# Sums of the down products' right operands formed in DRAM by accumulating transfers

## The chip, the cores and the metric

The kernel runs on one core of one Trainium2 chip. The metric is the device time of one execution in microseconds, lower being better; the time given for the kernel before is the median of three runs. The profile is of one further execution.

## The reference

One inference step of a hybrid decoder layer. What matters here are its two feed-forward halves, each over 1048 (first) or 1032 (second) tokens, with 1024 model dimensions and 2816 hidden features; everything is float32:

```python
def swiglu(x, wg, wu, wd):
    return (jax.nn.silu(x @ wg) * (x @ wu)) @ wd
...
    h = h + 0.5 * swiglu(rmsnorm(h, n1), w1g, w1u, w1d)
...
    h = h + 0.5 * swiglu(rmsnorm(h, n2), w2g, w2u, w2d)
```

Between the two stand an input projection, two recurrent scans (HGRN2 and Mamba-2) and an output projection. They are the same in both kernels.

## The kernel before, in words

Every large product is made of three TensorE passes (`mm3`, lines 166 to 171): both operands are split into a high part that TensorE can take exactly and a low rest, and high x high, high x low and low x high are added up. On top of that the FFN products are formed by a scheme of seven block products in place of eight: an operand is cut into two by two blocks, and the seven left and right operands are blocks or sums of blocks.

An FFN runs in `ffn` as a list of steps, each a chain of nine or twelve matmuls. `S.before(i, fn)` puts `fn`'s instructions ahead of step i, and this hand-made order holds for TensorE, VectorE, ScalarE and SyncE. GpSimd's queue is not in that list; its order follows the program.

**Gate and up products.** Eleven pairs i = 0 to 10 of 128-feature columns f = 2i and 2i + 1. `Plain` and `pair` make the first ones, `two_pairs` the other nine, each in 24 product steps of twelve matmuls and seven shorter chains of six. At a pair's end VectorE multiplies silu(gate) by up. That gives four gated blocks of 128 partitions by 524 columns: (f even, token half 0), called block 1; (f even, half 1), block 12; (f odd, half 0), block 2; (f odd, half 1), block 3. They are made at lines 621, 713 and 906, in two `s` buffers per pair.

**Right operands of the down products.** The seven operands are blocks 1, 2, 3 and the sums 5 = 12 - 1, 6 = 3 - 5, 7 = 3 - 12 and 4 = 2 - 6. `Hidden` keeps them in seven DRAM tensors, one for each operand. Per pair VectorE makes the four sums with `tensor_sub` (line 991) into two more `s` buffers, and SyncE stores all seven operands (line 994), 256 rows of 262 (or 258) floats each. `jobs` and `jobs_apart` place these: for the pairs of `two_pairs` the subtractions stand at steps s0 + 26, 32, 36 and 38, the stores at s0 + 19 to 41, so that some of them lie in the next pair or, for the last pair, in the first steps of the down products.

**Down products.** `down` runs through the operands in the order 1, 5, 6, 7, 3, 4, 2, with 24 steps for each. An operand is loaded from DRAM in three groups of pairs (0 to 3, 4 to 7, 8 to 10) and two token quarters (line 1023), cast on ScalarE (1027) and its rest formed on VectorE (1031). The down weights are loaded at line 1074, summed at 1084, split at 1089 and 1094. The first operand's products are evacuated by ScalarE (1114), those of the others are added by VectorE (1118), with a factor 0.5. SyncE issues its transfers strictly in order, so a store that waits for VectorE holds the loads behind it.

Of the kernel before, what the change touches and what calls it, by code (L numbers as in the profile page):

```python
# [13 lines left out]
ALU = mybir.AluOpType  # L14
# [553 lines left out]
def halves(t):  # L568
    return t.rearrange("p (c t) -> p c t", c=2)


def pair(K, S, wg, wu, f, ops, spread, hid, late_r, tight, first=None):

    nc = K.nc
    fs = slice(f * P, f * P + P)
    s0 = len(S.steps)  # L580
    tm = {}
    left = Left(K, [wg[:, 0:4, fs], wu[:, 0:4, fs], wu[:, 4:8, fs], wg[:, 4:8, fs]], 4)

    def temp(n, cs):
        if n not in tm:
            tm[n] = halves(K.t(2 * K.Q))
        return tm[n][:, cs]

    def times_r(n, i, cs, src=None):
        t = temp(n, cs)  # L590
        nc.vector.tensor_mul(t, t if src is None else src, spread.lanes(i, cs))
        return t

    def post(p, cs, b):
        if p == 1:
            nc.scalar.copy(temp("z", cs), b)
        elif p == 6:
            nc.vector.tensor_add(temp("v", cs), b, temp("z", cs))
        elif p == 2 and f == 0:
            nc.scalar.copy(temp("g0", cs), b)  # L600
        elif p == 2:
            t = times_r("g0", 0, cs, b)
            nc.scalar.activation(t, t, AF.Silu)
        elif p == 5:
            nc.vector.tensor_add(temp("x", cs), b, temp("v", cs))
        elif p == 7:
            nc.vector.tensor_add(temp("u1", cs), b, temp("x", cs))
        elif p == 3:
            nc.vector.tensor_add(temp("g1", cs), b, temp("v", cs))
        else:  # L610
            nc.vector.tensor_add(temp("u0", cs), b, temp("v", cs))

    def silu(n, cs):
        t = times_r(f"g{n}", n, cs)
        nc.scalar.activation(t, t, AF.Silu)

    def product_(n, cs):
        if "h" not in tm:
            tm["h"] = True
            hid.append(K.slot("s", K.T))  # L620
        nc.vector.tensor_mul(halves(hid[0][:, n * 2 * K.Q : n * 2 * K.Q + 2 * K.Q])[:, cs], temp(f"g{n}", cs), temp(f"u{n}", cs))

    if not first:
        left.plan(S, s0, int(tight), 5 * int(tight))
        Unit(K, left.w, [o.op for o in ops], 4, post).both(S)
        cs = slice(0, 2)
        for i, (fn, *args) in enumerate(((silu, 1, cs), (times_r, "u1", 1, cs), (times_r, "u0", 0, cs), (product_, 0, cs), (product_, 1, cs))):
            S.before(s0 + 12 + i, lambda fn=fn, args=args: fn(*args))
        return

    late = {}

    def post_first(p, cs, b):

        if p == 5:
            late[p] = b
        else:
            post(p, cs, b)
            if p == 6:
                post(5, cs, late[5])  # L640

    order = first(S, left)
    unit = Unit(K, left.w, [o.op for o in ops], 4, post_first)
    for ps_ in (order[:6], order[6:]):
        for c in range(2):
            for p in (1, 5, 6, 7, 2, 3) if c and len(ps_) == 6 else ps_:
                unit.step(S, p, c, (c,), True)
    cs = slice(0, 2)
    for i, (fn, *args) in enumerate(((silu, 0, cs), (silu, 1, cs), (times_r, "u0", 0, cs), (product_, 0, cs), (times_r, "u1", 1, cs), (product_, 1, cs))):
        S.before(s0 + late_r + i, lambda fn=fn, args=args: fn(*args))  # L650


class Plain:
# [44 lines left out]
    def late(self, S, at):  # L698
        nc = self.K.nc
        cs = slice(0, 2)  # L700

        def silu(n):
            g = self.g[n]
            nc.vector.tensor_mul(g, g, self.spread.lanes(n, cs))
            nc.scalar.activation(g, g, AF.Silu)

        def scale(n):
            u = self.u[n]
            nc.vector.tensor_mul(u, u, self.spread.lanes(n, cs))

        def times(n):
            out = halves(self.box()[:, n * 2 * self.K.Q : n * 2 * self.K.Q + 2 * self.K.Q])
            nc.vector.tensor_mul(out, self.g[n], self.u[n])

        for i, (fn, n) in enumerate(((silu, 0), (silu, 1), (scale, 0), (times, 0), (scale, 1), (times, 1))):
            S.before(at + i, lambda fn=fn, n=n: fn(n))
# [138 lines left out]
def two_pairs(K, S, wg, wu, i, ops, spread, hids, sub, before):  # L855
# [6 lines left out]
    nc = K.nc  # L862
    s0 = len(S.steps) - (0 if before else 2)
# [39 lines left out]
    def out(f, n):  # L903
        if not hids[f]:
            hids[f].append(K.slot("s", K.T))
        nc.vector.tensor_mul(halves(hids[f][0][:, n * 2 * K.Q : n * 2 * K.Q + 2 * K.Q]), temp(f, f"g{n}"), temp(f, ("v", "u1")[n]))

    def post(f, p, c):
        if p == 1:
# [53 lines left out]
GROUPS = [(0, 4), (4, 4), (8, 3)]  # L963


class Hidden:


# [1 line left out]
        self.K = K  # L970
        self.d = {p: K.dram.tile([P, 2, FP, self.K.Q], F32, name=K.uid("hd")) for p in ORDER}

    def parts(self, i, hid):

        K = self.K
        t, b = {}, {}

        def block(n):

            return hid[n // 2][0][:, n % 2 * 2 * self.K.Q : n % 2 * 2 * self.K.Q + 2 * self.K.Q]  # L980

        def val(p):
            return b[p] if p in b else block({1: 0, 12: 1, 2: 2, 3: 3}[p])

        def sub(p, x, y):
            s = {5: 0, 6: 0, 7: 1, 4: 1}[p]
            if s not in t:
                t[s] = K.slot("s", self.K.T)
            o = (p in (6, 4)) * 2 * self.K.Q
            b[p] = t[s][:, o : o + 2 * self.K.Q]  # L990
            K.nc.vector.tensor_sub(b[p], val(x), val(y))

        def store(p):
            K.nc.sync.dma_start(self.d[p][:, :, i, :], halves(val(p)))

        return sub, store

    def jobs(self, S, i, hid, e0, e1):

        sub, store = self.parts(i, hid)  # L1000
        for at, args in zip((e0 + 10, e1 + 3, e1 + 5, e1 + 8), ((5, 12, 1), (6, 3, 5), (7, 3, 12), (4, 2, 6))):
            S.before(at, lambda args=args: sub(*args))
            S.before(at + 2, lambda p=args[0]: store(p))
        for at, p in ((e0 + 2, 1), (e1 + 2, 2), (e1 + 3, 3)):
            S.before(at, lambda p=p: store(p))

    def jobs_apart(self, S, i, hid, s0):

        sub, store = self.parts(i, hid)
        for d, args in zip((26, 32, 36, 38), ((5, 12, 1), (6, 3, 5), (7, 3, 12), (4, 2, 6))):  # L1010
            S.before(s0 + d, lambda args=args: sub(*args))
        for d, p in zip((19, 29, 32, 33, 35, 39, 41), (1, 5, 3, 2, 6, 7, 4)):
            S.before(s0 + d, lambda p=p: store(p))

    def load(self, S, p, at):

# [23 lines left out]
def down(K, S, wdv, hidden, src, h, after):  # L1040
# [68 lines left out]
    def post(p, j, cs, b):  # L1109
        if p == 1:  # L1110
            tiles(j)
            for i in range(2):
                for n in range(2):
                    nc.scalar.mul(hs[2 * j + i][:, cs, n], b, 0.5)
            return
        for i, n in {5: ((0, 1), (1, 1)), 6: ((0, 1), (1, 0), (1, 1)), 7: ((1, 0), (1, 1)), 3: ((0, 1),), 4: ((1, 0),), 2: ((0, 0),)}[p]:
            t = hs[2 * j + i][:, cs, n]
            nc.vector.scalar_tensor_tensor(t, b, 0.5, t, ALU.mult, ALU.add)  # L1118
        for i, n in {3: ((0, 1), (1, 1)), 4: ((1, 0),), 2: ((0, 0),)}.get(p, ()):
            if then:  # L1120
                for c in range(cs.start, cs.stop):
                    then(2 * j + i, 2 * c + n)
# [41 lines left out]
def ffn(K, wg, wu, wd, ops, spread, src, first, after, late_r, at, plain=False):  # L1164
# [10 lines left out]
    with K.tc.manual_schedule(engines={E.PE, E.DVE, E.Activation, E.SP}):  # L1175
# [3 lines left out]
        if plain:  # L1179
            hid = [[], []]  # L1180
            lefts = [Left(K, [w[:, k : k + 4, f * P : f * P + P] for w, k in ((wgv, 0), (wuv, 0), (wuv, 4), (wgv, 4))], 4) for f in range(2)]
            first(S, *lefts)
            for f in range(2):
                p = Plain(K, lefts[f], ops, spread, hid[f], f == 1)
                p.add(S)
                p.late(S, late_r + 6 * f)
            hidden.jobs(S, 0, hid, late_r + 2, late_r + 10)
        sub = SubBlocks(K, ops)
        sub.jobs(S, at)
        before = None  # L1190
        for i in range(int(plain), NF // 2):
            hid, e = [], []
            if i > 1:
                hid = [[], []]
                s0, before = two_pairs(K, S, wgv, wuv, i, ops, spread, hid, sub, before)
                hidden.jobs_apart(S, i, hid, s0)
                continue
            for f in (2 * i, 2 * i + 1):
                hid.append([])
                pair(K, S, wgv, wuv, f, ops, spread, hid[-1], late_r, f == (2 if plain else 1), first if f == 0 else None)  # L1200
                e.append(len(S.steps))
            hidden.jobs(S, i, hid, *([late_r + 2, e[1]] if i == 0 else e))
        h = []
        down(K, S, wdv, hidden, src, h, after)
        S.run()
# [1362 lines left out]
```

## Time and profile before

| | |
|---|---|
| median of three runs | 1922.09 us (1920.74 to 1922.73) |
| span of the profiled execution | 1920.9 us |
| TensorE busy | 1905.5 us (99%) |
| VectorE busy | 1526.5 us (79%) |
| ScalarE busy | 858.0 us (45%) |
| GpSimd busy | 30.1 us (2%) |
| hardware queue of the DMA engines | 255.79 MB, 43.1% of 16 engines |
| software queue of the DMA engines | 0.04 MB |

The median lies 1.2 us above the span, which counts from the first instruction to the last. In the views PE is TensorE, PEld its weight load, DVE VectorE, ACT ScalarE, POOL GpSimd, SP or SPq SyncE, which issues the transfers. L991 is line 991. The first FFN's gate/up stage runs to about 473 us, its down products to about 690; the scans follow; the second FFN's gate/up stage ends near 1680 and its down products close the program. A row of a table by stretch gives, for each engine, the busy time and in brackets the number of instructions, then TensorE's clock, the share of the 16 DMA engines and GB/s.

### The profile page before, as it was taken

The page shows a single profiled execution, that of the slowest core. Times are in us where ns is not written, and L with a number is a line of the kernel's source. Part 1 is how long each engine was busy: PE and PEld are TensorE (multiplying, and loading weights), DVE is VectorE, ACT ScalarE, POOL GpSimd, SP SyncE. Part 2 cuts the span into 40 slices and gives each one's busy share as a digit, 9 for nine tenths or more (in the row PEclk, how much of TensorE's full clock was granted, in tenths as well). Part 3 has the DMA queues.
Part 4 walks back from the last instruction along what each step waited for, and adds up shares of the span by engine and source line. Part 5 has one row for each costly group of instructions (what it writes and reads, how often), then busy time and mean ns, then how long its engine had stood idle before and what let it go on. Part 6 is the DMA issues. An engine that isn't in the chain of part 4 may idle for free.

```text
span 1920.9 us, 41195 instructions
## 1 busy us (share of the span) xinstructions
PE 1905.5 (99%) x16692; PEld 1875.2 (98%) x16692; DVE 1526.5 (79%) x2866; ACT 858.0 (45%) x1635; POOL 30.1 (2%) x88
## 2 busy tenths in 40 slices
PE   9999999999999999999999999999999999999998
PEld 9999999999999999999999999999999999999998
DVE  7888888889788877566585557999888888978974
ACT  6533333334534644466564545743333332453353
POOL 3000000000000000000000000000000000000000
PEclk9999999999999999999999999999999999999999
DMA  7143333335967541221463254133333333596852
GB/s 249 50 128 95 95 107 112 92 98 175 305 215 243 165 152 52 66 89 38 116 186 85 83 173 144 58 114 107 99 93 101 101 112 93 173 269 210 281 175 84
DMA packets 324209, 258.46 MB, mean 135 GB/s; under 512 B 18923, under 2 KB 298731, under 8 KB 324011
## 3 DMA queue, kind: packets, MB, share of 16 engines
q1 hardware_dynamic: 323779, 255.79, 43.1%
q8 instruction: 131, 2.15, 0.5%
q14 instruction: 59, 0.48, 0.1%
q0 software_dynamic: 224, 0.04, 0.0%
q10 hardware_dynamic: 16, 0.00, 0.0%
HBM read 190.79 MB, written 65.05 MB: 133 GB/s over the span
## 4 chain that ended last, share of the span: by engine, by line
PE 94%; DVE 3%; ACT 1%; issue 1%; DMA 0%; SPq 0%; DVEq 0%; ACTq 0%
PE acc L169 24%; PE acc L171 23%; PE acc L170 23%; PE mis L169 5%; PE mis L170 5%; PE mis L171 5%; PE mis L1963 1%; DVE u L382 1%; DVE u L367 1%; PE mis L1665 0%; PE mis L2030 0%; PE mis L1659 0%; DMA s<-in_x_prompt_dram 0%; PE mis L2055 0%; PE mis L1654 0%
## 5 line engine op out<-in xcount | busy, mean ns | idle before, releaser
L169 PE MATMUL acc<-u,ws 128*128 128x258 f32 (+4 forms) x3634 | 1064.0, 293 | 1.1 <-DVE u L1279 0.8
L171 PE MATMUL acc<-u,ws 128*128 128x258 f32 (+4 forms) x3634 | 1055.3, 290 | 0.7 <-DVE ws L501 0.7
L170 PE MATMUL acc<-u,ws 128*128 128x258 f32 (+4 forms) x3634 | 1054.8, 290 | 0.0
L169 PEld LDWEIGHTS acc<-u,ws 128*128 128x128 f32 x3634 | 686.5, 189 | 8.7 <-issue 6.2
L170 PEld LDWEIGHTS acc<-u,ws 128*128 128x128 f32 x3634 | 688.3, 189 | 0.8 <-DVE u L330 0.2
L171 PEld LDWEIGHTS acc<-u,ws 128*128 128x128 f32 x3634 | 686.1, 189 | 1.6 <-DVE ws L501 1.1
L169 PE MATMUL mis<-u,ws 128*128 128x262 f32 (+1 forms) x810 | 230.2, 284 | 0.0
L171 PE MATMUL mis<-u,ws 128*128 128x262 f32 (+1 forms) x810 | 228.7, 282 | 0.0
L170 PE MATMUL mis<-u,ws 128*128 128x262 f32 (+1 forms) x738 | 208.6, 283 | 0.0
L501 DVE TENSOR_TENSOR ws<-r,ws 128x512 fp32r<-128x512 f32 x266 | 181.6, 684 | 4.1 <-ACT ws L497 3.9
L901 ACT ACTIVATE t<-t 128x524 f32<-128x524 f32 (+1 forms) x72 | 46.1, 640 | 300.1 <-DVE t L898 300.1
L497 ACT CAST ws<-r 128x512 fp32r<-128x512 f32 x266 | 156.8, 615 | 42.2 <-PE mis L171 18.1
L169 PEld LDWEIGHTS mis<-u,ws 128*128 128x128 f32 x810 | 152.9, 189 | 0.1
L171 PEld LDWEIGHTS mis<-u,ws 128*128 128x128 f32 x810 | 152.7, 189 | 0.0
L170 PEld LDWEIGHTS mis<-u,ws 128*128 128x128 f32 x738 | 139.9, 190 | 0.1
L493 DVE TENSOR_TENSOR r<-r,r 128x512 f32<-128x512 f32 x150 | 100.8, 684 | 0.3
L1031 DVE TENSOR_TENSOR u<-u,u 128x1048 fp32r<-128x1048 f32 (+3 forms) x84 | 96.1, 1146 | 4.8 <-ACT u L1027 4.3
L1089 ACT CAST ws<-u 128x512 fp32r<-128x512 f32 (+1 forms) x72 | 42.1, 585 | 109.9 <-DVE u L1084 105.2
L164 DVE TENSOR_TENSOR ws<-r,ws 128x512 fp32r<-128x512 f32 x88 | 59.5, 685 | 38.3 <-ACT ws L163 38.0
L1027 ACT CAST u<-u 128x1048 fp32r<-128x1048 f32 (+3 forms) x84 | 82.8, 988 | 1.3 <-DMA u<-hd 1.3
L1118 DVE SCALAR_TENSOR_TENSOR s<-acc,s 128x524 f32<-128x524 f32 (+3 forms) x86 | 53.9, 651 | 35.3 <-PE acc L171 35.0
L898 DVE TENSOR_TENSOR t<-t,u 128x524 f32<-128x524 f32 (+1 forms) x108 | 73.2, 692 | 0.1
(465 smaller groups left out, 2329.1 us busy)
## 6 DMA issues: line engine op xcount, KB each, us to landing
r<-in_w_ffn_down_dram SPq DMA_DIRECT2D x128, 256.0 KB
hd<-s SPq DMA_DIRECT2D x93, 258.0 KB
r<-in_w_ffn_gate_dram SPq DMA_DIRECT2D x88, 256.0 KB
r<-in_w_ffn_up_dram SPq DMA_DIRECT2D x88, 256.0 KB
hd<-s SPq DMA_DIRECT2D x77, 262.0 KB
u<-hd SPq DMA_DIRECT2D x36, 516.0 KB
u<-hd SPq DMA_DIRECT2D x28, 524.0 KB
r<-in_w_in_dram SPq DMA_DIRECT2D x56, 256.0 KB
```

The lines of the kernel that those rows point to most:

```text
L164: self.nc.vector.tensor_sub(lo, src, hi.bitcast(F32))
L169: mm(ps, whi, xhi, start=first, stop=False, skip_group_check=more)
L170: mm(ps, whi, xlo, start=False, stop=False, skip_group_check=more)
L171: mm(ps, wlo, xhi, start=False, stop=last, skip_group_check=more)
L493: self.K.nc.vector.tensor_tensor(self.raw[p], self.raw[x], self.raw[y], op)
L497: self.K.nc.scalar.copy(self.w[p][:, : self.n * P], self.raw[p])
L501: self.K.nc.vector.tensor_sub(t[:, 512 : 512 + w], self.raw[p], t[:, :w].bitcast(F32))
L898: nc.vector.tensor_mul(t, t if src is None else src, spread.lanes(n, slice(0, 2)))
L901: nc.scalar.activation(t, t, AF.Silu)
L1027: K.nc.scalar.copy(hi, lo.bitcast(F32))
L1031: K.nc.vector.tensor_sub(lo, lo.bitcast(F32), hi.bitcast(F32))
L1118: nc.vector.scalar_tensor_tensor(t, b, 0.5, t, ALU.mult, ALU.add)
```

## The change

VectorE no longer forms the four sums. SyncE stores each gated block, as soon as it is made, into the operands whose sum begins with it, and GpSimd then issues accumulating transfers that add the later blocks to the same DRAM tensors. So that all are additions, blocks 12 and 2 are made with a minus sign, by `scalar_tensor_tensor` with -1 in place of `tensor_mul`; operands 5, 4 and 2 come out with the opposite sign, and the factor 0.5 of their results becomes -0.5. Per pair that is seven stores by SyncE as before, and seven accumulations by GpSimd.

```diff
+def gated(K, f, n, out, g, u):
+    if f % 2 != n:
+        K.nc.vector.scalar_tensor_tensor(out, g, -1.0, u, ALU.mult, ALU.mult)
+    else:
+        K.nc.vector.tensor_mul(out, g, u)
...
+PARTS = (((1, 5, 6, 4), ()), ((7,), (5, 6, 4)), ((2,), (4,)), ((3,), (7, 6, 4)))
+SIGN = {5: -1, 4: -1, 2: -1}
...
-            K.nc.vector.tensor_sub(b[p], val(x), val(y))
-
-        def store(p):
-            K.nc.sync.dma_start(self.d[p][:, :, i, :], halves(val(p)))
...
+    def put(self, i, hid, n):
+        src = halves(hid[n // 2][0][:, n % 2 * 2 * K.Q : n % 2 * 2 * K.Q + 2 * K.Q])
+        for p in PARTS[n][0]:
+            K.nc.sync.dma_start(self.d[p][:, :, i, :], src)
+        for p in PARTS[n][1]:
+            K.nc.gpsimd.dma_start(self.d[p][:, :, i, :], src, accum_op=ALU.add)
...
-            nc.vector.scalar_tensor_tensor(t, b, 0.5, t, ALU.mult, ALU.add)
+            nc.vector.scalar_tensor_tensor(t, b, 0.5 * SIGN.get(p, 1), t, ALU.mult, ALU.add)
...
-                hidden.jobs_apart(S, i, hid, s0)
+                hidden.jobs(S, i, hid, s0 + 19, s0 + 27, s0 + 31, s0 + 33)
```

SyncE's queue at the end of the first FFN's last pair, before. hd_109 is operand 1 in DRAM, hd_110 operand 6, hd_111 2, hd_112 5, hd_113 7, hd_114 3, hd_115 4; s_ are the gated blocks and sums, r_ down weights, u_ loaded operands:

```order
L994 DMA hd_109<-s_5746 256x1x262
L1074 DMA r_5778<-in_w_ffn_down_dram 128x4x128
L1023 DMA u_5805<-hd_109 128x786
L1023 DMA u_5834<-hd_109 128x786
L1074 DMA r_5837<-in_w_ffn_down_dram 128x4x128
L1074 DMA r_5873<-in_w_ffn_down_dram 128x3x128
L1074 DMA r_5909<-in_w_ffn_down_dram 128x4x128
L1074 DMA r_5946<-in_w_ffn_down_dram 128x4x128
L1023 DMA u_5966<-hd_112 128x1048
L994 DMA hd_112<-s_5925 256x1x262
```

The same place after the change, from the row behind the store into hd_109:

```order
L990 DMA hd_112<-s_5756 256x1x262
L990 DMA hd_110<-s_5756 256x1x262
L990 DMA hd_115<-s_5756 256x1x262
L1058 DMA r_5791<-in_w_ffn_down_dram 128x4x128
L1007 DMA u_5818<-hd_109 128x786
L1007 DMA u_5847<-hd_109 128x786
L1058 DMA r_5850<-in_w_ffn_down_dram 128x4x128
L1058 DMA r_5886<-in_w_ffn_down_dram 128x3x128
L1058 DMA r_5922<-in_w_ffn_down_dram 128x4x128
L990 DMA hd_113<-s_5756 256x1x262
L1058 DMA r_5961<-in_w_ffn_down_dram 128x4x128
L1007 DMA u_5981<-hd_112 128x1048
```

Four stores of the pair's first block, that into hd_109 and the three at the top, now go out together ahead of the last loads of operand 1, and the first load of operand 5 (u_5966 before, u_5981 now) has moved behind the store that SyncE waits at: before it is the store of a difference, now that of the second gated block. One weight load (r_5961) has moved behind it as well.

GpSimd's queue for the same last pair, after; before, no transfer stands there and its next row is the memset with which the scans' preparation begins:

```order
L992 DMA hd_112<-s_5756 256x1x262
L992 DMA hd_110<-s_5756 256x1x262
L992 DMA hd_115<-s_5756 256x1x262
L992 DMA hd_115<-s_5995 256x1x262
L992 DMA hd_113<-s_5995 256x1x262
L992 DMA hd_110<-s_5995 256x1x262
L992 DMA hd_115<-s_5995 256x1x262
```

The second block is added to operands 5, 6 and 4, the third to 4, the fourth to 7, 6 and 4. An accumulation into a tensor waits for the store or the accumulation before it into the same rows, and GpSimd issues strictly in order.

More of the change, by code (lines that the diff above doesn't have):

```diff
@@ L620, in product_ @@
             hid.append(K.slot("s", K.T))
-        nc.vector.tensor_mul(halves(hid[0][:, n * 2 * K.Q : n * 2 * K.Q + 2 * K.Q])[:, cs], temp(f"g{n}", cs), temp(f"u{n}", cs))
+        gated(K, f, n, halves(hid[0][:, n * 2 * K.Q : n * 2 * K.Q + 2 * K.Q])[:, cs], temp(f"g{n}", cs), temp(f"u{n}", cs))
     if not first:
@@ L712, in times @@
             out = halves(self.box()[:, n * 2 * self.K.Q : n * 2 * self.K.Q + 2 * self.K.Q])
-            nc.vector.tensor_mul(out, self.g[n], self.u[n])
+            gated(self.K, int(self.keep), n, out, self.g[n], self.u[n])
         for i, (fn, n) in enumerate(((silu, 0), (silu, 1), (scale, 0), (times, 0), (scale, 1), (times, 1))):
@@ L905, in out @@
             hids[f].append(K.slot("s", K.T))
-        nc.vector.tensor_mul(halves(hids[f][0][:, n * 2 * K.Q : n * 2 * K.Q + 2 * K.Q]), temp(f, f"g{n}"), temp(f, ("v", "u1")[n]))
+        gated(K, f, n, halves(hids[f][0][:, n * 2 * K.Q : n * 2 * K.Q + 2 * K.Q]), temp(f, f"g{n}"), temp(f, ("v", "u1")[n]))
     def post(f, p, c):
@@ L971, in __init__, with jobs @@
         self.d = {p: K.dram.tile([P, 2, FP, self.K.Q], F32, name=K.uid("hd")) for p in ORDER}
-    def parts(self, i, hid):
+    def put(self, i, hid, n):
         K = self.K
[L976 to L991, printed above, removed]
-        def store(p):
[L994 to L1013, printed above, removed]
+        src = halves(hid[n // 2][0][:, n % 2 * 2 * K.Q : n % 2 * 2 * K.Q + 2 * K.Q])
[3 more added lines that the diff above has]
+            K.nc.gpsimd.dma_start(self.d[p][:, :, i, :], src, accum_op=ALU.add)
+    def jobs(self, S, i, hid, *at):
+        for n, d in enumerate(at):
+            S.before(d, lambda n=n: self.put(i, hid, n))
     def load(self, S, p, at):
@@ L1186, in ffn @@
                 p.late(S, late_r + 6 * f)
-            hidden.jobs(S, 0, hid, late_r + 2, late_r + 10)
+            hidden.jobs(S, 0, hid, late_r + 5, late_r + 7, late_r + 11, late_r + 13)
         sub = SubBlocks(K, ops)
@@ L1201, in ffn @@
                 e.append(len(S.steps))
-            hidden.jobs(S, i, hid, *([late_r + 2, e[1]] if i == 0 else e))
+            e0, e1 = (late_r + 2, e[1]) if i == 0 else e
+            hidden.jobs(S, i, hid, e0 + 4, e0 + 5, e1 + 4, e1 + 5)
         h = []
```

## The prediction

> **What bounds the kernel now.** I read the page's totals first, then busy time per 40 us, then TensorE's own waits. The page gives the span and each engine's total:
>
> ```profile
> span 1920.9 us, 41195 instructions
> PE 1905.5 (99%) x16692; PEld 1875.2 (98%) x16692; DVE 1526.5 (79%) x2866; ACT 858.0 (45%) x1635; POOL 30.1 (2%) x88
> ```
>
> TensorE has 15.4 us of idle time in the whole span. No relief of another engine can return more than that. GpSimd (POOL) is nearly unused. Next are four 40 us stretches; the columns are PE, PEld, DVE, ACT, POOL, the clock, the DMA share and GB/s:
>
> ```profile
> 80.00:120.00 40.00, 39.41 (x319) 38.78 (x318) 39.15 (x64) 13.86 (x25) 0.00 (x0) 1.00 0.37 115
> 320.00:360.00 40.00, 40.00 (x331) 40.00 (x330) 34.64 (x64) 12.89 (x24) 0.00 (x0) 1.00 0.33 101
> 480.00:520.00 40.00, 40.00 (x330) 40.00 (x329) 29.42 (x43) 25.18 (x41) 0.00 (x0) 1.00 1.00 300
> 1240.00:1280.00 40.00, 39.66 (x324) 38.99 (x323) 38.96 (x63) 24.68 (x44) 0.00 (x0) 1.00 0.33 107
> ```
>
> In the steady gate/up stage (320 to 360) TensorE is never idle and runs a matmul each 40/331 = 0.121 us, with VectorE 87% busy beside it: VectorE is near its limit there, but under it. Only where an FFN begins (80 to 120, 1240 to 1280) is VectorE full and TensorE short, by 0.59 and 0.34 us. Where the down products begin (480 to 520) TensorE is full and the DMA engines are too. The change takes work from the first kind of place and gives work to the second. TensorE's direct waits on the weight splits agree that the first kind is small:
>
> ```profile
> PE acc L171 <- DVE ws L501: 0.7, 2, 0.4
> ```
>
> **The subtractions that go, the products that get a sign.** The groups of instructions give counts and means:
>
> ```profile
> L991 DVE TENSOR_TENSOR s<-s,s 128x524 f32<-128x524 f32 (+1 forms) x66 | 45.7, 692 | 0.1
> L991 DVE TENSOR_TENSOR s<-s 128x524 f32<-128x524 f32 (+1 forms) x22 | 15.3, 694 | 0.0
> L906 DVE TENSOR_TENSOR s<-t,t 128x524 f32<-128x524 f32 (+1 forms) x72 | 50.4, 700 | 3.5
> L1512 DVE SCALAR_TENSOR_TENSOR u<-u,col,u 128x1040 f32<-128x1040 f32 x24 | 31.1, 1294 | 0.0
> L382 DVE TENSOR_TENSOR u<-u,u 128x1048 fp32r<-128x1048 f32 (+1 forms) x30 | 36.9, 1236 | 7.8 <-ACT u L376 7.7
> ```
>
> Removed: 88 subtractions, 45.7 + 15.3 = 61.0 us of VectorE. Of the 88 gated products, 44 become a scalar-tensor-tensor. That form takes 1.294 us on 1040 columns where the plain product takes 1.236 on 1048, so I add 0.06 us each: 44 x 0.06 = 2.6 us. VectorE falls by 58 us, to about 1468. The turned signs in the down products change only a constant in an instruction that stands already: nothing.
>
> How much of the 58 us does TensorE see? Only what falls where it is short. In pieces of 5 us, a full one being 5.00 and 43 or 44 matmuls:
>
> ```profile
> 85.00:90.00 5.00, 4.56 (x38) 4.35 (x37) 5.00 (x9) 0.00 (x0) 0.00 (x0) 1.00 0.15 54
> 105.00:110.00 5.00, 4.95 (x41) 4.77 (x40) 5.00 (x9) 0.00 (x0) 0.00 (x0) 1.00 0.09 28
> 110.00:115.00 5.00, 4.89 (x40) 4.71 (x39) 4.39 (x8) 3.20 (x6) 0.00 (x0) 1.00 0.67 187
> ```
>
> The chain of waits, for the first of them, and then VectorE's first subtraction of each FFN:
>
> ```profile
> 85.99 0.61 DVE s L713
> 86.60 0.61 DVE ws L501
> 87.26 0.39 PE acc L171
> 90.18 0.70 DVE L991 TENSOR_TENSOR s<-s 128x524 f32<-128x524 f32 x1
> 1286.96 0.69 DVE L991 TENSOR_TENSOR s<-s 128x516 f32<-128x516 f32 x1
> ```
>
> This stall lies behind a gated product (L713) and before the first subtraction, at 90.18, so nothing removed shortens it; two of the products ahead of it get a sign, so it grows by 2 x 0.06 = 0.1 us. The Trainium skill ("Vector Engine (DVE) Microarchitecture Reference", Points that are easy to get wrong) says of this form that two non-bf16 SBUF sources halve its throughput. The L1512 row speaks against it (1.24 ns an element, against 1.18 for the plain product); by the page the two products would cost some 1.1 us here instead of 0.1. The other two pieces come after four removed subtractions. Their shortage is 0.16 us by busy time and 7 matmuls, 0.85 us, by count; I take 0.5 as the gain. In the second FFN the first subtraction stands at 1286.96, behind the short stretch (1240 to 1280), so I take nothing there. Sum for VectorE: -0.5 + 0.1 = **-0.4 us**, bounds -0.85 and +0.1.
>
> **The accumulating transfers.** Per pair SyncE still issues seven stores. GpSimd adds seven transfers of the same size that read their target, add and write: 154 in all. The trace has none, so I bound one. A plain store, alone in its 4 us (the issue, then the stretch):
>
> ```profile
> 335.96 0.52 SPq L994 DMA_DIRECT2D hd<-s  x1
> 336.00:340.00 4.00, 4.00 (x35) 4.00 (x35) 1.66 (x3) 1.31 (x3) 0.00 (x0) 1.00 0.19 67
> 460.10 0.52 SPq L994 DMA_DIRECT2D hd<-s  x1
> 463.19 0.81 SPq L1023 DMA_DIRECT2D u<-hd  x2
> ```
>
> It fills the 16 engines for 0.19 x 4 = 0.76 us: the low bound. The high bound is a whole round trip, from a store's issue to the load that waits for it: 463.19 - 460.10 = 3.1 us. An accumulation reads two blocks and writes one, about a store and a load: I take 1.6 us (estimate, twice 0.76). For GpSimd's issue the nearest row is a small transfer at the start:
>
> ```profile
> 2.92 0.54 POOL L1234 DMA_DIRECT2D t<-in_conv_w_dram  x1
> ```
>
> Its 32 rows take 0.54 us. With 256 rows I allow 0.54 to 8 x 0.54 = 4.3 us and take 1. In one pair TensorE has 24 x 12 + 7 x 6 = 330 matmuls, 39.9 us. Seven accumulations are 11.2 us of DMA in that (21.7 at most) beside 0.33 x 40 = 13.2 now: 0.61 of the engines, 0.87 at most. GpSimd needs 7 us, 30 at most. Both fit, and the weight loads there are early: they wait for a free buffer, and VectorE never waits for them in that stage.
>
> ```profile
> SPq L487 <- DVE ws L501: 257.3, 86, 9.9
> ```
>
> So the steady stage costs nothing.
>
> **The start of the down products** is the place that decides. The last pair's accumulations fall there. DMA share per 4 us of the first FFN:
>
> ```profile
> 472.00:476.00 4.00, 4.00 (x36) 4.00 (x35) 4.00 (x9) 3.17 (x5) 0.00 (x0) 1.00 0.05 18
> 476.00:480.00 4.00, 4.00 (x35) 4.00 (x34) 3.97 (x7) 0.92 (x2) 0.00 (x0) 1.00 0.57 160
> 480.00:484.00 4.00, 4.00 (x35) 4.00 (x34) 3.65 (x7) 3.76 (x8) 0.00 (x0) 1.00 0.57 206
> 484.00:488.00 4.00, 4.00 (x35) 4.00 (x34) 3.78 (x6) 2.60 (x4) 0.00 (x0) 1.00 0.76 180
> 488.00:492.00 4.00, 4.00 (x36) 4.00 (x35) 1.55 (x3) 3.04 (x6) 0.00 (x0) 1.00 1.03 378
> 528.00:532.00 4.00, 4.00 (x35) 4.00 (x35) 3.24 (x6) 2.97 (x4) 0.00 (x0) 1.00 0.50 117
> ```
>
> From 488 to 528 the engines are full; whatever is added before delays every load in it. Free before that: 4 x (0.95 + 0.43 + 0.43 + 0.24) = 8.2 us. SyncE's order changes too. Now it stands at a store for a subtraction, until 476.08; after, at the store of the product that ends at 473.9, with a load of block 5 (1.6 us of DMA) queued behind it that used to go out at 466.93:
>
> ```profile
> 466.93 2.52 SPq L1023 DMA_DIRECT2D u<-hd  x1
> 476.08 0.52 SPq L994 DMA_DIRECT2D hd<-s  x1
> 495.25 0.56 SPq L1023 DMA_DIRECT2D u<-hd  x1
> 473.19 0.69 DVE L906 TENSOR_TENSOR s<-t,t 128x524 f32<-128x524 f32 x1
> 481.52 0.71 DVE L906 TENSOR_TENSOR s<-t,t 128x524 f32<-128x524 f32 x1
> ```
>
> Three stores move ahead to 460, -2.3 us. Added: 7 x 1.6 + 1.6 - 2.3 = 10.5 us; 2.3 us more than is free. What cover has TensorE? ACT evacuates the first product's four groups, and VectorE makes the second product's last operand:
>
> ```profile
> 480.83 2.39 ACT L1114 ACTIVATE s<-acc 128x524 f32<-128x524 f32 x4 [0.17 <-PE acc L171]
> 505.25 2.38 ACT L1114 ACTIVATE s<-acc 128x524 f32<-128x524 f32 x4
> 504.55 0.97 DVE L1031 TENSOR_TENSOR u<-u,u 128x786 fp32r<-128x786 f32 x1
> ```
>
> Three groups last 24.4 us, so a group takes 8.1 and the second product starts at 505.0. Its first group's last step (after 57 of 66 matmuls) needs that operand at 512.0; it is ready at 505.5. Cover: 6.5 us, against 2.3 us of delay. Cost taken: **0**. The accumulation of block 5 is issued near 475 and its load at 495; those of blocks 6, 7 and 4 are loaded later still, so no wait for data opens.
>
> **Rivals.** (a) *The DMA engines at the start of the down products.* With c us per accumulation the delay is 7c - 0.7 - 8.2; it passes the cover of 6.5 at c = 2.2, and 0.2% of the time in both FFNs together at c = 2.5. At c = 3.1 it is 12.8, so TensorE waits 6.3 us in each FFN, 12.6 in all, span about 1933. For it: the full stretch, and a cost that is unmeasured. Against it: two reads and a write make 1.6. The Trainium skill ("DMA: Bandwidth & Descriptors", Issuing engines are not separate DMA queues) says that transfers from all issuing engines run on the same 16 engines and interleave, which is this rival's mechanism; the second queue buys nothing there. Chance 0.25. (b) *GpSimd becomes a queue.* The waits of its in-order queue (each accumulation for the store or the accumulation before it on the same block, and for its own completion slots) make one take over 39.9/7 = 5.7 us. At 7 us it falls behind by 9 us a pair, 82 us over nine pairs; the load of block 5 then blocks SyncE some 55 us beyond the cover, in both FFNs: near 2030 us. Against: the bound of 4.3. Chance 0.04. (c) *VectorE's backlog was the real bound of the fronts,* and its relief returns the idle time there, 0.59 + 0.34, and through earlier starts some 4 of the 15.4 us of all. Against: the stalls come before the subtractions. Chance 0.03; about 1917.
>
> **How the numbers follow.** The profiled span is 1920.9; the median of the runs is 1922.1, so 1.2 us lie around it. Forecast: 1920.9 - 0.4 + 0 + 1.2 = **1921.7 us**, chance 0.68. What can be told from no change is 0.2%, 3.8 us. Faster by more: rival (c), 0.03. Slower by more: (a) and (b), 0.29. Range: from 1919.0 (a few tenths beyond -0.85, and part of (c)) to rival (a) at its bound, 1921.7 + 12.6 = 1934.3; beyond it lie (b), half of (c) and the dearest part of (a), under 0.2.
>
> **What would show it.** Right: L991 gone, VectorE near 1468 us busy; TensorE idle time within 1 us of now; a software queue of some 40 MB; DMA share near 0.6 in the steady stage and TensorE full at 488 to 540. Wrong: TensorE waiting for L1031 or L1094 near 505 to 530 (a); SyncE waiting at L1023 for the accumulations, GpSimd issues that slip pair by pair (b); scalar-tensor-tensor products over 1.2 us; a front that is shorter by microseconds (c).

## The result and the profile after

The changed kernel takes **1953.15 us** (median of four runs, 1952.24 to 1953.42) against 1921.41 us for the kernel before on the same chip: ratio 1.0157, interval 1.0143 to 1.0171. It is 31.7 us slower; the forecast was 1921.7 us, in a range up to 1934.3. The profiled span grew from 1920.9 to 1951.7 us. One of the ten runs of the fifth kernel below took 3696.62 us; the time given there is the median of the other nine.

The page of the changed kernel, its totals and GpSimd's queue of transfers:

```profile
span 1951.7 us, 41510 instructions
PE 1908.4 (98%) x16692; PEld 1878.2 (96%) x16692; DVE 1476.5 (76%) x2778; ACT 858.7 (44%) x1635; POOL 197.7 (10%) x242
q0 software_dynamic: 42112, 41.05, 17.7%
```

VectorE is 50 us less busy, and TensorE has as many matmuls as before, but its idle time rose from 15.4 to 43.3 us. The stretches of 40 us say where (columns as before: PE, PEld, DVE, ACT, POOL, clock, DMA share, GB/s):

```profile
80.00:120.00 40.00, 39.57 (x325) 39.32 (x324) 37.00 (x60) 13.86 (x25) 7.71 (x7) 1.00 0.79 171
320.00:360.00 40.00, 40.00 (x331) 40.00 (x331) 32.45 (x60) 12.89 (x24) 7.58 (x7) 1.00 0.74 148
480.00:520.00 40.00, 32.11 (x264) 31.90 (x262) 16.52 (x22) 18.01 (x29) 5.72 (x6) 0.94 1.01 258
520.00:560.00 40.00, 32.70 (x251) 32.70 (x252) 27.53 (x42) 14.77 (x23) 1.08 (x1) 0.85 0.83 241
1720.00:1760.00 40.00, 26.79 (x212) 26.59 (x211) 15.28 (x25) 12.09 (x21) 4.36 (x4) 0.83 0.82 200
```

The last two stretches before the change:

```profile
520.00:560.00 40.00, 40.00 (x331) 40.00 (x330) 31.82 (x47) 14.53 (x21) 0.00 (x0) 1.00 0.71 224
1720.00:1760.00 40.00, 40.00 (x335) 40.00 (x334) 32.65 (x50) 16.01 (x23) 0.00 (x0) 1.00 0.92 288
```

At the front and in the steady stage TensorE does as forecast. The loss lies at the start of the down products, in both FFNs. TensorE's waits, then ScalarE's in the first FFN's stretch and in the second's, name the chain (who waits, for whom; total, times, longest):

```profile
PE acc L169 <- ACT s L1098: 28.4, 2, 15.2
```

```profile
ACT s L1098 <- DMA hd<-s: 19.4, 1, 19.4
```

```profile
ACT s L1098 <- DMA hd<-s: 18.3, 1, 18.3
```

L1098 is ScalarE's evacuation of the first down product into the `h` tiles (L1114 before). It waits for a transfer that *reads* an `s` buffer: one of GpSimd's accumulations. The timelines of ScalarE and of GpSimd show which (start, duration, engine, line, count, idle before and its releaser):

```profile
505.40 1.25 ACT L1098 ACTIVATE s<-acc 128x524 f32<-128x524 f32 x2
526.00 1.25 ACT L1098 ACTIVATE s<-acc 128x524 f32<-128x524 f32 x2 [19.36 <-DMA hd<-s]
```

```profile
479.20 1.08 POOL L992 DMA_DIRECT2D hd<-s  x1 [5.26 <-DVE s L575]
486.58 1.09 POOL L992 DMA_DIRECT2D hd<-s  x1 [6.30 <-issue]
494.57 1.08 POOL L992 DMA_DIRECT2D hd<-s  x1 [6.90 <-issue]
503.25 1.09 POOL L992 DMA_DIRECT2D hd<-s  x1 [7.60 <-DVE u L1015]
510.50 1.08 POOL L992 DMA_DIRECT2D hd<-s  x1 [6.15 <-issue]
516.27 1.09 POOL L992 DMA_DIRECT2D hd<-s  x1 [4.70 <-issue]
521.02 1.08 POOL L992 DMA_DIRECT2D hd<-s  x1 [3.65 <-issue]
```

These are the last pair's seven accumulations. Each takes 1.1 us to issue, but they go out five to nine us apart. From issue to landing a transfer takes 4.9 us (median of the 154; 4.3 to 9.1), so the last lands near 526, when the second evacuation begins. There are eight `s` buffers, and `down` takes eight of them for its `h` tiles, so the eighth tile gets the buffer that holds blocks 2 and 3 of the last pair. Before, the readers of such a buffer were VectorE's subtractions and plain stores; now the last four of GpSimd's transfers are among them. ScalarE stands at that evacuation, TensorE waits for the accumulator behind it, and the casts behind it in ScalarE's queue stop VectorE too:

```profile
508.00:512.00 4.00, 4.00 (x34) 3.90 (x33) 0.00 (x0) 0.00 (x0) 1.08 (x1) 1.00 1.13 333
512.00:516.00 4.00, 0.11 (x1) 0.00 (x0) 0.00 (x0) 0.00 (x0) 0.00 (x0) 0.88 0.75 146
520.00:524.00 4.00, 0.00 (x0) 0.00 (x0) 0.00 (x0) 0.00 (x0) 1.08 (x1) 0.50 0.38 30
528.00:532.00 4.00, 4.00 (x20) 4.00 (x20) 2.68 (x5) 1.13 (x2) 0.00 (x0) 0.50 0.46 122
532.00:536.00 4.00, 4.00 (x35) 4.00 (x34) 3.37 (x7) 1.52 (x3) 0.00 (x0) 0.99 1.00 311
```

After the stall TensorE runs 20 matmuls in 4 us instead of 35, at a granted clock of 0.50: 15 x 0.114 = 1.7 us lost on top. After the second FFN's stall it is 28 instead of 36, 8 x 0.111 = 0.9 us:

```profile
1752.00:1756.00 4.00, 4.00 (x28) 4.00 (x27) 2.60 (x6) 1.13 (x2) 0.00 (x0) 0.74 0.54 136
```

So the loss adds up, within half a microsecond: 28.4 of waiting + 2.6 of slow clock - 0.7 (six matmuls more at the front) = 30.3 us, against 30.8 between the spans.

Theory T: the whole loss is the release of that `s` buffer, because GpSimd's accumulations go out one at a time. Open were why they do, and whether late loads, the steady stage or GpSimd's backlog have a part in it.

### The profile page after: what moved, and what is told of

Its sections match the earlier page's. It is cut to its first block, busy times and chain, and to the rows that moved or that the text cites. A ratio compares the mean times of both kernels' runs of the same rounds, so it can differ in the third digit from the quotient of the medians.

```text
span 1951.7 us, 41510 instructions
## 1 busy us (share of the span) xinstructions
PE 1908.4 (98%) x16692; PEld 1878.2 (96%) x16692; DVE 1476.5 (76%) x2778; ACT 858.7 (44%) x1635; POOL 197.7 (10%) x242
## 3 DMA queue, kind: packets, MB, share of 16 engines
q0 software_dynamic: 42112, 41.05, 17.7%
## 4 chain that ended last, share of the span: by engine, by line
PE 90%; DVE 3%; issue 3%; DMA 2%; ACT 2%; POOL 0%; SPq 0%; DVEq 0%; ACTq 0%; POOLq 0%
PE acc L169 23%; PE acc L171 22%; PE acc L170 22%; PE mis L169 5%; PE mis L170 5%; PE mis L171 5%; DMA hd<-s 1%; DMA u<-hd 1%; DVE u L382 1%; PE mis L1948 1%; DVE u L367 1%; PE mis L1650 0%; PE mis L2015 0%; PE mis L1644 0%; DMA s<-in_x_prompt_dram 0%
## 5 line engine op out<-in xcount | busy, mean ns | idle before, releaser
L169 PE MATMUL acc<-u,ws 128*128 128x258 f32 (+4 forms) x3634 | 1065.8, 294 | 29.3 <-ACT s L1098 28.4
L992 POOL DMA_DIRECT2D hd<-s x154 | 167.5, 1088 | 965.1 <-issue 395.4
L1015 DVE TENSOR_TENSOR u<-u,u 128x1048 fp32r<-128x1048 f32 (+3 forms) x84 | 96.0, 1145 | 7.4 <-ACT u L1011 6.6
L1078 DVE TENSOR_TENSOR ws<-u,ws 128x512 fp32r<-128x512 f32 (+1 forms) x72 | 46.2, 642 | 59.6 <-ACT ws L1073 59.6
```

The costliest lines, as they stand in the source:

```text
L169: mm(ps, whi, xhi, start=first, stop=False, skip_group_check=more)
L992: K.nc.gpsimd.dma_start(self.d[p][:, :, i, :], src, accum_op=ALU.add)
L1015: K.nc.vector.tensor_sub(lo, lo.bitcast(F32), hi.bitcast(F32))
L1078: nc.vector.tensor_sub(t[:, 512 : 512 + n * P], box[0], t[:, : n * P].bitcast(F32))
```

## The experiments

The ratio given for each is to the kernel before on the same chip, with its 95% interval. For the first four kernels the kernel before took 1921.69 us, for the next four 1922.07, then 1921.61 and 1922.55.

**1. The last pair by VectorE.** `sums` stands for the old subtractions and stores, with the signs turned (5 = block 1 + block 12, and so on).

```diff
-                hidden.jobs(S, i, hid, s0 + 19, s0 + 27, s0 + 31, s0 + 33)
+                if i < 10:
+                    hidden.jobs(S, i, hid, s0 + 19, s0 + 27, s0 + 31, s0 + 33)
+                else:
+                    hidden.sums(S, i, hid, [s0 + d for d in (26, 32, 36, 38)], ...)
```

> The last pair (i = 10) of each FFN has its four sums formed by VectorE and stored by SyncE at the steps of the kernel before; the other ten pairs keep the accumulating transfers. Theory T (the whole loss is the two waits of ScalarE's first evacuation into the last h tiles for the s buffer that the last pair's accumulations still read): TensorE's wait behind the evacuation at the first down product falls from 28.4 us to under 1 us and the time to 1921 to 1923, ratio to before 0.999 to 1.001. Rival S (the 140 accumulations of the other pairs cost time in the steady stage or through later loads): a good part of the 31 us stays, 1930 to 1950.

Measured: 1920.57 us, ratio 0.9994 (0.9985 to 1.0004), a little under the range expected. TensorE's longest wait anywhere is 1.7 us, for the load of an input. The whole loss hangs on 14 of 154 accumulations; the other 140 cost nothing that can be measured. Rival S falls.

**2. Only the last pair accumulates:** the same edit with `if i == 10`.

> The reverse: only the last pair of each FFN uses accumulating transfers, the other ten have their sums formed by VectorE. Theory T (the last pair's own seven transfers, one every 6 to 9 us from 479 on, outlast the buffer): the loss stays whole, 1949 to 1954. Rival Q (GpSimd's queue is late because of what nine pairs have left in it): it starts empty here, the last transfer is issued 10 us earlier or more and most of the loss goes, 1922 to 1938.

Measured: 1948.62 us, ratio 1.0141 (1.0126 to 1.0156). TensorE's wait (L1126 is the evacuation here):

```profile
PE acc L169 <- ACT s L1126: 23.3, 2, 12.2
```

GpSimd's queue is empty when the last pair comes, and most of the loss is still there: 27 of 31.7 us, just under the range that theory T gave. The last transfer goes out at 518.16 instead of 521.02, not the 10 us earlier that rival Q needs. Backlog accounts for the 5 us by which the wait is shorter, no more.

**3. Twice the memory for descriptors.**

```diff
-    nc = _bacc.Bacc("TRN2", target_bir_lowering=False, num_devices=1, dynamic_dma_scratch_size=1024)
+    nc = _bacc.Bacc("TRN2", target_bir_lowering=False, num_devices=1, dynamic_dma_scratch_size=2048)
```

> The changed kernel with the memory set aside for GpSimd's transfer descriptors doubled, 1024 to 2048 bytes, nothing else. Theory A (one transfer of 256 rows fills the descriptor memory, so GpSimd cannot issue the next until it has drained): transfers into different tensors follow at under 2 us instead of 5.3, the idle time of GpSimd put down to issue falls from 395 us below 150, the last pair's seven are out by 505 and the wait in the down products is gone, 1920.5 to 1923. Theory B (an accumulating transfer cannot overlap the next one, whatever the memory): nothing changes, 1951 to 1954.

Measured: 1921.08 us, ratio 0.9999 (0.9989 to 1.0008). GpSimd's timeline over the last pair, all of it, and the stretch:

```profile
474.27 3.28 POOL L992 DMA_DIRECT2D hd<-s  x3 [24.16 <-DVE s L575]
487.12 3.30 POOL L992 DMA_DIRECT2D hd<-s  x3 [9.57 <-DMA hd<-s]
495.55 1.07 POOL L992 DMA_DIRECT2D hd<-s  x1 [5.13 <-DMA hd<-s]
```

```profile
480.00:520.00 40.00, 40.00 (x331) 40.00 (x329) 23.51 (x34) 21.59 (x36) 4.37 (x4) 1.00 1.11 297
```

Three go out back to back, and the last is issued at 495.55 instead of 521.02. What GpSimd still waits for are the accumulations before into the same rows, no longer its own issue. Theory B falls: accumulating transfers do overlap. The Trainium skill ("DMA: Bandwidth & Descriptors", SWDGE vs HWDGE vs iDMA) says that GpSimd writes the descriptors of its transfers into rings in a piece of SBUF set aside. With nothing but the size set for the descriptors doubled, 1953.15 us became 1921.08.

**4. Plain transfers in place of accumulating ones.**

```diff
-            K.nc.gpsimd.dma_start(self.d[p][:, :, i, :], src, accum_op=ALU.add)
+            K.nc.gpsimd.dma_start(self.d[p][:, :, i, :], src)
```

> The seven transfers per pair by GpSimd are plain stores over the same rows instead of accumulations, so operands 5, 6, 7 and 4 hold only the last block written to them; queue, sizes, order and waits are those of the changed kernel. If the reading and adding makes a transfer slow (part of theory B): landing falls from 4.9 to under 3.5 us, they follow each other at under 4 us and the wait is gone, 1921 to 1924. Theory A: still one at a time, landing 3.5 to 4.9 us each, at least half of the wait stays, 1935 to 1953.

Measured: 1920.57 us, ratio 0.9993 (0.9983 to 1.0002): the wait is gone, against what theory A was said to give. The page's line for GpSimd's queue (packets, MB, share of the engines) shows why this doesn't tell the theories apart:

```profile
q0 software_dynamic: 12544, 41.05, 6.5%
```

The same bytes go in 12544 packets instead of 42112, (42112 - 12544)/154 = 192 fewer per transfer. A plain transfer is cheaper to hold as well as to carry out: with the old 1024 bytes three of them go out in 2.13 us. My expectation had taken both to be alike; the run is inconclusive on the cost of adding.

**5. Another buffer, the same queue.**

```diff
+        if last and f:
+            hids[f].append(temp(f, f"g{n}"))
+            gated(K, f, n, hids[f][n], hids[f][n], temp(f, ("v", "u1")[n]))
+            return
         if not hids[f]:
             hids[f].append(K.slot("s", K.T))
```

> The changed kernel with one buffer moved: in the last pair of each FFN blocks 2 and 3 are multiplied in place in their gate temporaries (t tiles) instead of into an s buffer, so that none of the eight h tiles takes the buffer that the last four accumulations read. GpSimd's queue, its transfers, their sources' sizes and the descriptor memory are untouched. Theory T (the release of that buffer is what TensorE waits for): the last accumulation still lands near 525, ScalarE no longer waits for it, the 28.4 us are gone and the time is 1920.5 to 1924. Rival L (the late accumulations matter in themselves, by filling the DMA engines or by holding the loads of the operands behind them): TensorE waits at about the same place for a cast or a weight split instead, 1930 to 1953.

Measured: 1920.96 us, ratio 0.9997 (0.9988 to 1.0006). GpSimd's last accumulations, ScalarE's evacuation, and the two stretches:

```profile
514.12 1.09 POOL L999 DMA_DIRECT2D hd<-t  x1 [6.55 <-issue]
522.41 1.08 POOL L999 DMA_DIRECT2D hd<-t  x1 [7.20 <-issue]
```

```profile
504.66 2.38 ACT L1105 ACTIVATE s<-acc 128x524 f32<-128x524 f32 x4
```

```profile
480.00:520.00 40.00, 40.00 (x330) 40.00 (x330) 25.39 (x36) 24.52 (x39) 5.44 (x5) 1.00 1.12 302
520.00:560.00 40.00, 40.00 (x331) 40.00 (x331) 33.27 (x49) 14.53 (x21) 1.08 (x1) 1.00 0.82 252
```

The accumulations are as late as in the changed kernel, one at a time, the last issued even later (522.41), and nobody waits: the four evacuations run through, as before the change. So lateness alone costs nothing; the buffer it holds does. This run by itself shows that the wait is for the release of that buffer (theory T), and rival L falls.

**6. Half as much more descriptor memory:** as in 3, with 1536.

> The changed kernel with 1536 bytes for GpSimd's transfer descriptors, between the 1024 of the change and the 2048 that were enough. Theory A (the memory holds so many transfers of 256 rows; one at 1024, three or more at 2048): transfers go out in twos, the last pair's last one is issued near 505 instead of 521, and most of the wait goes: 1921 to 1930. If the memory only counts in powers of two, it behaves as 1024: 1951 to 1954.

Measured: 1921.57 us, ratio 0.9995 (0.9986 to 1.0004). GpSimd over the last pair:

```profile
473.06 2.19 POOL L992 DMA_DIRECT2D hd<-s  x2 [21.18 <-DVE s L575]
480.71 1.09 POOL L992 DMA_DIRECT2D hd<-s  x1 [5.47 <-issue]
490.06 2.18 POOL L992 DMA_DIRECT2D hd<-s  x2 [8.26 <-DMA r<-in_w_ffn_down_dram]
497.98 1.09 POOL L992 DMA_DIRECT2D hd<-s  x1 [5.74 <-issue]
500.27 1.08 POOL L992 DMA_DIRECT2D hd<-s  x1 [1.21 <-issue]
```

One at 1024, two at 1536, three at 2048: theory A, and no counting in powers of two. With twos the last goes out at 500.27; with 5.9 us from issue to landing (median in this kernel) it lands near 506.2, and the evacuation needs the buffer near 506.6 (526.00 - 19.36 in the changed kernel). So 1536 bytes are enough with little to spare.

**7. The signs alone:** `sums` for all pairs, no accumulation.

> One part of the change alone: the signs are turned (44 gated products as scalar-tensor-tensor, factor -0.5 for three operands), but VectorE forms all sums as before and SyncE stores them at the steps of before; no accumulating transfer is left. The turned products measured 0.699 us, the plain ones beside them 0.699: 1920.5 to 1922.5, no difference to before, and VectorE 1526 to 1528 us busy. If the form cost 0.06 us more where VectorE is late, still within 0.3 us of that.

Measured: 1922.71 us, ratio 1.0004 (0.9995 to 1.0013). The turned signs cost nothing.

**8. Both cures:** VectorE in the last pair, 2048 bytes.

> Both cures together, as the version most likely to be faster than before: accumulating transfers in ten pairs, VectorE in the last, and 2048 bytes of descriptor memory. By theory T the relief is the front's only, 0.4 to 0.9 us: 1920.5 to 1921.5, ratio 0.9990 to 1.0000. Rival V (the 50 us taken from VectorE are worth something once nothing is late): 1915 to 1919.

Measured: 1921.42 us, ratio 0.9997 (0.9988 to 1.0006). Rival V falls. No version here is shown to be faster than the kernel before: the five with accumulations and without the stall (1, 3, 5, 6, 8) have ratios of 0.9994 to 0.9999, with 1 in every interval.

**9 and 10. More load on the DMA engines, first try.** Base: kernel 5 with 2048 bytes.

```diff
+        if i == 6 and n == 3:
+            for t in self.spare:
+                K.nc.gpsimd.dma_start(t, self.d[1][:, :, 0, :])
+        if i == FP - 1:
+            for _ in range({1: 7, 3: 0}.get(n, 0)):
+                K.nc.gpsimd.dma_start(self.spare.pop(), self.d[1][:, :, 0, :], accum_op=ALU.add)
```

> What the DMA engines can still take at the start of the down products. Blocks 2 and 3 of the last pair in t tiles as in the fifth kernel, 2048 bytes of descriptor memory, and in the last pair seven more accumulating transfers of the same size, right behind the three of block 12, into spare tensors in DRAM that nothing reads (spare tensors are filled in the seventh pair by plain transfers); the outputs are those of the reference. An accumulation costs 1.9 us of the 16 engines by the third kernel (15.1% of 1920.6 us over 154). Theory P (the prediction's account: a delay of added DMA time less 8.2 us free and 6.5 us of cover): 7 x 1.9 + 1.6 - 2.3 - 8.2 = 4.4 us of delay without the extra ones, 17.7 with them, 11 us of waiting in each FFN, about 1944. Rival M (the loads of this stretch are issued well ahead of their use and share the engines with the extra ones, so the cover is larger): 1921 to 1926.

> The same with seven further ones behind the last pair's last accumulation, fourteen extra in all. Theory P: 31 us of delay, 24.5 us of waiting in each FFN, about 1970. Rival M: the second seven fall behind the first product, where the share of the engines drops again; some wait appears, 1922 to 1945.

Measured: 1935.01 us, ratio 1.0068 (1.0053 to 1.0083), and 1947.16 us, ratio 1.0128 (1.0111 to 1.0145). Neither bears on its question: the extra transfers depend on nothing but the first pair's rows, and they run at the front of each FFN (from 80 to 124 us and from 1284 to 1326 in the ninth kernel). The text ahead of the prediction says that GpSimd's order follows the program; for transfers that depend on nothing later it doesn't. The front of the first FFN in the ninth kernel:

```profile
80.00:120.00 40.00, 33.46 (x264) 33.02 (x263) 29.97 (x49) 11.40 (x22) 16.36 (x19) 0.95 1.13 227
```

TensorE is 55 matmuls short of the 319 of before, 6.6 us. The share of the DMA engines is 1.13 (0.79 in the changed kernel), and VectorE waits 7.5 us for a gate weight: the front has no room for that much more.

**11 and 12. The same at its place:** the extra transfers read operand 2's rows of the last pair, which are stored near 485.

```diff
-                K.nc.gpsimd.dma_start(t, self.d[1][:, :, 0, :])
+                K.nc.gpsimd.dma_start(t, self.d[2][:, :, i, :])
...
-            for _ in range({1: 7, 3: 0}.get(n, 0)):
-                K.nc.gpsimd.dma_start(self.spare.pop(), self.d[1][:, :, 0, :], accum_op=ALU.add)
+            for _ in range({2: 7}.get(n, 0)):
+                K.nc.gpsimd.dma_start(self.spare.pop(), self.d[2][:, :, i, :], accum_op=ALU.add)
```

> The ninth kernel with its extra transfers at the place they were meant for: their source is now the last pair's rows of operand 2, so that they cannot be issued before about 485; seven accumulations into spare tensors then run beside the loads of the second product (spare tensors filled in the steady stage; the outputs are those of the reference). Theory P (what is added is delay beyond 6.5 us of cover): 4.4 + 7 x 1.9 = 17.7 us of delay, 11 us of waiting in each FFN, 1940 to 1946. Rival M (more cover than the prediction counted): 1921 to 1926.

> The same with fourteen extra accumulations. Theory P: 31 us of delay, 24.5 us of waiting in each FFN, near 1970. Rival M: the wait begins somewhere between seven and fourteen, 1922 to 1945; it stands at a cast, a weight split or a load behind a late accumulation.

Measured with seven: 1940.61 us, ratio 1.0098 (1.0083 to 1.0113). TensorE's wait, VectorE ahead of it, and the stretches around the first (L1029 forms an operand's low part; it is L1031 before and L1015 in the changed kernel; L1082 sums two down weights):

```profile
PE acc L170 <- DVE u L1029: 10.0, 2, 5.6
```

```profile
516.26 0.69 DVE L1082 TENSOR_TENSOR u<-r,r 128x512 f32<-128x512 f32 x1 [5.56 <-DMA r<-in_w_ffn_down_dram]
```

```profile
508.00:512.00 4.00, 4.00 (x35) 4.00 (x34) 1.92 (x3) 1.37 (x2) 1.17 (x2) 1.00 1.18 259
512.00:516.00 4.00, 0.34 (x3) 0.13 (x2) 0.00 (x0) 0.00 (x0) 1.90 (x2) 1.00 1.20 234
516.00:520.00 4.00, 2.11 (x8) 1.81 (x8) 2.87 (x4) 2.90 (x6) 0.00 (x0) 0.62 1.20 254
520.00:524.00 4.00, 4.00 (x20) 4.00 (x20) 2.41 (x4) 0.97 (x2) 0.00 (x0) 0.53 1.11 300
```

With fourteen: 1960.23 us, ratio 1.0200 (1.0183 to 1.0217), and TensorE waits for that line and for the evacuations of the second product on VectorE (L1116):

```profile
PE acc L169 <- DVE s L1116: 16.3, 5, 5.9
PE acc L170 <- DVE u L1029: 8.1, 2, 5.7
```

Theory P's time holds for seven (1940 to 1946 expected) and is too dear for fourteen (near 1970), but its sum holds for neither: TensorE waits 10.0 us in all with seven, where P had 11 us in each FFN, and some 24 us with fourteen, where P had 24.5 in each. That the time with seven agrees is in part luck: of the 17.2 us by which that span is longer (1938.1 against 1920.9) 6.6 are not waiting: TensorE is busy 1912.1 us with the same matmuls (1902.6 to 1905.8 in the kernels without a stall), at a granted clock of 0.53 to 0.62 after the wait. What comes late is not the operand either: VectorE stands at the weight sum, which waits for a down weight, and forms the operand's low part right behind it. By the profile SyncE waits no more than 0.7 us in this stretch for a transfer into the operands, so it is the load on the engines and not GpSimd's order that makes the weights late. Rival M falls with seven. So a contention of the DMA engines is there to be had, at the place and the moment (512) that the prediction's rival (a) named; the change's own seven accumulations stay under the cover.

## Why the prediction was wrong, step by step

- **VectorE: -58 us, to 1468.** Measured -50.0, to 1476.5. The signs were not the error. They are free; the groups of the changed kernel are equal:

```profile
L577 DVE TENSOR_TENSOR s<-t,t 128x516 f32<-128x516 f32 (+1 forms) x43 | 30.0, 699 | 1.3
L575 DVE SCALAR_TENSOR_TENSOR s<-t,t 128x516 f32<-128x516 f32 (+1 forms) x43 | 30.0, 699 | 2.4
```

  So the 0.06 us for each was too much (it was read off rows of 1040 columns and put on products of 524), and the rule of the Trainium skill weighed there ("Vector Engine (DVE) Microarchitecture Reference", Points that are easy to get wrong) doesn't show at all. The groups that went had the 61.0 us of durations that were counted, but the busy time counts once what overlaps between neighbours (before, the durations of all of VectorE's groups add up to 1679.6 us, at 1526.5 us busy) and fell by 50.0: a subtraction of 0.694 us frees 0.57 us. A difference of busy time is to be read from busy time; here nothing hung on it.
- **The front: -0.4 us.** The first FFN's stretch gained six matmuls, 0.7 us, within the bounds given, and no run could tell it from nothing.
- **An accumulation: 1.6 us of the 16 engines, 1 us of GpSimd.** 17.7% of 1951.7 us over 154 is 2.2 us, and 1.9 us in kernel 3 (15.1% of 1920.6); the issue is 1.09 us. Both inside the bounds. The share of the DMA engines in the steady stage is 0.74, not 0.61, and under the bound of 0.87.
- **"GpSimd needs 7 us, 30 at most."** Failed. It counted the issue alone. With 1024 bytes of descriptor memory an accumulation must drain before the next is issued (kernels 3 and 6); the changed kernel's group says it in its idle time:

```profile
L992 POOL DMA_DIRECT2D hd<-s x154 | 167.5, 1088 | 965.1 <-issue 395.4 <-DVE r L493 198.4 <-DVE s L575 84.7
```

  395.4 us of idle time put down to issue. In the steady stage one goes out in some 5.3 us (the middle value of the distances from 120 to 470 us), so seven need 37 of a pair's 39.9 us, beyond the bound of 30. This is the mechanism of rival (b), kept just under its threshold of 5.7 us. Among the full DMA engines of the down products the distance grows to as much as 8.7 us.
- **The steady stage costs nothing.** Right (kernel 1).
- **The start of the down products costs 0.** This is the step that failed, in its sentence "so no wait for data opens". It followed the accumulations to those who read what they write, the loads of the operands, and never to those who need the buffer that they read. Its answer on the DMA engines held: TensorE stays full with all accumulations on (kernels 3, 5 and 6), and seven more open a wait at the forecast moment (kernel 11). The sizes in that sum held less well: with 2.2 us an accumulation, as in kernel 5, its own delay is 7 x 2.2 - 0.7 - 8.2 = 6.5 us, the whole cover, and in kernel 11 the wait is less than half of what the sum gives. So that this zero came out has some luck in it. Rival (a) and the cost of zero were both worked out on the right place and the wrong resource.
- **The rivals.** None named the release of the `s` buffer. Of the three, only (b) had a cause that took part.

## What to carry to other kernels

A transfer is a reader: when work moves from an engine to a queue, list who next allocates each buffer that the queue reads, and when the last transfer out of it lands, not only who needs the result. For transfers that GpSimd issues, take the distance between two from the landing time unless the descriptor memory is known to hold several; 512 bytes more of it took the whole loss of 31.7 us away. Relieving an engine that has 13% of slack, and that the bounding engine hardly waits for, gives nothing: 50 us less of VectorE moved no run by more than its interval.

## What was not expected of the hardware

- Two or three accumulations of 256 rows of 1048 or 1032 bytes in flight cost less of the engines than one at a time: 1.9 us each with three, 2.0 with two (16.2% of 1918.8 us over 154), 2.2 alone. An accumulating transfer makes 192 packets more than a plain one of the same bytes, and the plain one takes 6.5% of 1918.7 us over 154, 0.81 us.
- TensorE comes out of a stall at half clock: 20 matmuls in 4 us after 15.2 us of waiting (changed kernel, 528 to 532), and 20 in 4 us after 5.6 us (kernel 11, 520 to 524). The Trainium skill ("TensorE: Matmul & The Clock Gate", Part 1) gives a window of about 3.4 us, idle or busy, for either change of the clock; the records agree with its order of size: in the changed kernel the mean clock of 0.88 from 512 to 516 puts the fall some 3 us after the stall's start, and full clock is back near 532, some 5 us after the first matmul at 527.3. By the matmuls missing in these stretches a stall is some 1 to 3 us dearer than its wait.
- Why a plain transfer makes 80 packets where an accumulating one makes 272 stays open (the counts fit 154 x 80 + 224 and 154 x 272 + 224), and so does the cost of the adding by itself.
